# Seven block products for eight pairs of gated units in the second layer of a two-layer decoder step

## The chip, the cores and the metric

The kernel runs on one core of a Trainium2 chip. The metric is the device time of one execution in microseconds (us); lower is better. In the profile PE is TensorE's matmul side and PEld its weight loads, DVE is VectorE, ACT is ScalarE, POOL is GpSimd, and SP is the engine that issues most DMAs.

## The reference, cut to what matters

Two layers run over 520 positions (512 of a prompt, 8 single-position samples) with 1024 channels. The first layer is a convolution mixer; the change leaves its arithmetic alone. The second is a gated MLP with a spatial mix:

```python
def c_mixer(x, w_in, w_s, b_s, norm_v_g, norm_v_b, w_out):
    z = jnp.einsum('bld,de->ble', x, w_in)          # D_MODEL 1024 -> 3 x 2048
    u, v, g = jnp.split(z, (D_C, 2 * D_C), axis=-1)
    u = jax.nn.gelu(u)
    v = layer_norm(jax.nn.gelu(v), norm_v_g, norm_v_b)
    ...
    w_causal = w_s * jnp.tril(jnp.ones((CHUNK, CHUNK), w_s.dtype))
    mix = jnp.einsum('hts,bnshd->bnthd', w_causal, vc) + jnp.transpose(b_s)[None, None, :, :, None]
    ...
    y = u * mix * jax.nn.silu(g)
    return jnp.einsum('ble,ed->bld', y, w_out), v

# every layer: x <- LayerNorm(alpha * x + sublayer(x))
```

All data are fp32.

## The kernel before, in words

**Layout.** Channels lie on the 128 partitions and positions on the free axis, so an activation of 1024 channels is eight tiles of 128 x 520. The weights come as *units*: 1024 input channels by 128 output channels, a tile of 128 x 1024 in SBUF, one DMA of 512 KB each. There are 136 units, in the order in which they are used: first layer 0 to 71 (the last eight, 64 to 71, are its second output projection), then v 72 to 87, then for each half of the 2048 gated channels four u, four g, four u, four g (88 to 103 and 112 to 127), and eight units of the output projection (104 to 111, 128 to 135).

**Exact products.** Each fp32 operand is split into two fp32r parts, a rounded one (`whi`, `x1h`) and the rest (`wlo`, `x1l`). `whi` is a cast on ACT (L121), `wlo` a subtraction on DVE (L128); for units 10 to 49 it is an accumulating DMA instead. A product of a unit takes three matmuls (hi by hi, lo by hi, hi by lo) for each of 8 blocks of input channels and each half of 260 positions: 48 matmuls of 128x128 by 128x260, in `mm2` (L157). `mm` (L142) does one half of the positions, 24 matmuls.

**Order.** `unit(n)` (L137) sees to it that the weights of the next `LEAD` = 5 units have been asked for. The parts live in 12 slots of the tag W; the raw weights in 3 of the tag `raw`. The instruction order of every engine is laid down by the framework when the kernel is built, by priorities (program order, raised by `soon()`, lowered by `background()`) and by its own estimate of times. On the chip each engine runs its list in order and waits on semaphores; a slot is taken again when its last reader is done. SP's queue, which issues all raw loads, is such a list too.

**PSUM.** `zps` holds two tiles of two banks (`zt`), `cps` two of one bank, `mps` two for small things such as transposes and mixes.

**Second layer.** Sixteen v units: product, GELU, then `v_tok` (L616): four transposes on TensorE, an ACT copy to an SBUF tile (L622), statistics on DVE. All 16 transposed tiles stay in SBUF (in slots that the first layer used for `cA` and `sB`). `v_finish` (L655), called after the first u unit, makes mean and scale and normalizes the 64 blocks of v in place on DVE (L663). `c_group` (L733) does four u units (GELU on ACT, L741, into `gu`) and then four g units (SiLU on ACT, L756). `mix_unit` (L710) is eight small matmuls on v and a DVE pass (L722); `split_y` makes the product with `mix` (L405) and its two fp32r parts (ACT cast L406, DVE L407), `yh` and `yl`. After eight channel blocks, `z_q` multiplies them by the output projection and the partial sums stay in SBUF as `r1` (L773, L776). After the other eight, `out_part` (L478 on) does the second projection (`z_p`) in two halves of the positions, adds it to the kept sum on DVE (L492), and normalizes.

The temporaries have tags of their own: T (`tmp`, 7 slots), B (`btmp`, 4 slots, which hold `gu`), Y (17 slots), M (4 slots).

Of the kernel before, what the change touches and what calls it, by code (L numbers as in the profile page):

```python
# [9 lines left out]
F32 = mybir.dt.float32  # L10
# [31 lines left out]

LEAD = 5
CUT = 260
# [6 lines left out]
def decoder_kernel(  # L51
# [27 lines left out]
    zps = ctx.enter_context(tc.tile_pool(name="zps", bufs=2, space=bass.MemoryType.PSUM))  # L79
    mps = ctx.enter_context(tc.tile_pool(name="mps", bufs=2, space=bass.MemoryType.PSUM))  # L80

    def xs_slot(dt, name):
# [4 lines left out]

    def ab_slot(name):
        return slots.tile([P, T], F32, tag="AB", name=name, bufs=8)

# [21 lines left out]

    n_units = 2 + wu.shape[0]
    units = [None, None]

    def load_unit(wtag=("W", 12)):
        n = len(units)
        raw = wpool.tile([P, KT, P], F32, tag="raw", name=f"raw_{n}", bufs=3)
        nc.sync.dma_start(raw, wu[n - 2])
        hi = wpool.tile([P, KT, P], F32R, tag=wtag[0], name=f"whi_{n}", bufs=wtag[1])  # L120
        nc.scalar.copy(hi, raw)  # L121
        lo = wpool.tile([P, KT, P], F32R, tag=wtag[0], name=f"wlo_{n}", bufs=wtag[1])
        if n in BY_DMA:

            nc.scalar.mul(lo, raw, -1.0)  # L125
            nc.gpsimd.dma_start(lo, wu[n - 2], accum_op=ALU.add)  # L126
        else:
            nc.vector.tensor_tensor(lo, raw, hi.bitcast(F32), op=ALU.subtract)  # L128
        units.append((hi, lo))


    BY_DMA = set(range(10, 50))
    EXTRA = set()
    for base in (64, 128):
        EXTRA.update((base + 6, base + 7))

    def unit(n):  # L137
        while len(units) < min(n + 1 + LEAD, n_units):
            load_unit(("M", 4) if len(units) in EXTRA else ("W", 12))
        return units[n]  # L140

# [14 lines left out]

    def mm2(z, w, ah, al):  # L157
        hi, lo = w
        for k in range(KT):
            for h in range(2):  # L160
                for j, (a, b) in enumerate(((hi, ah), (lo, ah), (hi, al))):
                    nc.tensor.matmul(  # L162
                        z[h][:, :TH],
                        a[:, k, :],
                        b[k][:, hs(h)],
                        start=(k == 0 and j == 0),
                        stop=(k == KT - 1 and j == 2),
                    )
# [15 lines left out]
    for k in range(KT):  # L184
        x = tmp(f"x_{k}")
        if k % 4 == 0:
            raw = wpool.tile([P, 4, 2, P], F32, tag="raw", name=f"raw_s{k}", bufs=3)
            w0h.append(wpool.tile([P, 4, 2, P], F32R, tag="W", name=f"whi_s{k}", bufs=12))
            w0l.append(wpool.tile([P, 4, 2, P], F32R, tag="W", name=f"wlo_s{k}", bufs=12))
        q, j = k // 4, k % 4  # L190
# [28 lines left out]

    load_unit()  # L220
    pa = const.tile([P, KT, NPA], F32, name="pa")
# [13 lines left out]


    unit(1)
    xs = []
    for j in range(2):
        t = wpool.tile([P, 4, NS, WA], F32, tag="M", name=f"xs_{j}", bufs=4)  # L240
        nc.sync.dma_start(t, cache_a[:, 4 * j : 4 * j + 4])
        xs.append(t)
# [45 lines left out]
    for i in range(KT):  # L288
# [24 lines left out]
        nc.gpsimd.dma_start(cap_out[:, i, :], ap[:, SEQ : SEQ + PADA])  # L313
        cA.append(ab_slot(f"cA_{i}"))
        if i % 2 == 1:
# [16 lines left out]
        nc.gpsimd.dma_start(cbp_out[:, i, :], ch[:, SEQ : SEQ + PADB])  # L332
        s = slots.tile([P, T], F32, tag="SB", name=f"sB_{i}", bufs=8)
        sB.append(s)
# [24 lines left out]
    with background():  # L359
        for j in range(2):  # L360
            nc.gpsimd.dma_start(cas_out[:, 4 * j : 4 * j + 4], xs[j])
            proda = wpool.tile([P, 4, NS, WA], F32, tag="M", name=f"proda_{j}", bufs=4)
# [95 lines left out]
    for d in range(KT):  # L458
        xr = tmp(f"xr_{d}")
        nc.sync.dma_start(xr, xT[:, d, :])  # L460
        r = slots.tile([P, T], F32, tag="SB", name=f"r_{d}", bufs=8)
        if d == 2:
# [15 lines left out]
    def out_part(base, c0, c1, yh, yl, res, lnc, done, last=False, pool_sub=()):  # L478
# [39 lines left out]
        def norm():  # L518
# [26 lines left out]
            for d in range(KT):  # L545
# [3 lines left out]
                if last:  # L549
                    if d % 4 == 0:  # L550
                        out = wpool.tile([P, 4, nn], F32, tag="raw", name=f"out_{d}", bufs=3)
                    o = out[:, d % 4, :]
# [38 lines left out]

    wt = wpool.tile([P, NH, P], F32, tag="M", name="wt", bufs=4)
    nc.gpsimd.dma_start(wt, wsT_in)
    bs = wpool.tile([P, NH, P], F32, tag="M", name="bs", bufs=4)
    nc.gpsimd.dma_start(bs, bs_in)
# [17 lines left out]
    vs = tiny.tile([P, NV, NS], F32, name="vs")  # L613
    stats = wpool.tile([P, NC, NV, 6], F32, tag="M", name="stats", bufs=4)

    def v_tok(i):  # L616
        nc.gpsimd.tensor_copy(vs[:, i, :], vt[i][:, SEQ:])
        m = mt(f"vt_{i}")
        for c in range(NC):
            nc.tensor.transpose(m[:, c * P : (c + 1) * P], vt[i][:, c * P : (c + 1) * P], ident)  # L620
        t = ab_slot(f"vtok_{i}") if i < 8 else slots.tile([P, T], F32, tag="SB", name=f"vtok_{i}", bufs=8)
        nc.scalar.copy(t[:, :SEQ], m)  # L622
# [19 lines left out]
    for i in range(NVF, NV):  # L642
        z = zt(f"z_v{i}")
        mm2(halves(z), unit(n + i), x1h, x1l)
        vt[i] = y_slot(F32, f"v_{i}")
        nc.scalar.activation(two(vt[i]), zh(z), AF.Gelu_apprx_tanh)
        v_tok(i - 1)
    n += NV

    mv = tiny.tile([P, NC, 2], F32, name="mv")  # L650
    rs = tiny.tile([P, NC], F32, name="rs")
    mixs = tiny.tile([P, NV, NS], F32, name="mixs")
    rowsum = wpool.tile([P, NH, P], F32, tag="M", name="rowsum", bufs=4)

    def v_finish():  # L655
# [4 lines left out]
        nc.gpsimd.tensor_tensor(rs, rs, neg_half[:, :NC], op=ALU.pow)  # L660
        for i in range(NV):
            for c in range(NC):
                nc.vector.tensor_scalar(  # L663
                    vtok[i][:, c * P : (c + 1) * P],
                    vtok[i][:, c * P : (c + 1) * P],
                    mv[:, c, 0:1],
                    rs[:, c : c + 1],
                    op0=ALU.subtract,
                    op1=ALU.mult,
                )  # L670

# [37 lines left out]

    def mix_unit(i):  # L710
        h = i // 2
# [5 lines left out]
        for c in range(NC):  # L717
            nc.tensor.matmul(  # L718
                m[:, c * P : (c + 1) * P], vtok[i][:, c * P : (c + 1) * P], wt[:, h, :], start=True, stop=True
            )  # L720
# [10 lines left out]
        return t  # L731

    def c_group(g0):  # L733
        nonlocal n
        gu = []
        for i in range(g0, g0 + 4):
            z = zt(f"z_u{i}")
            mm2(halves(z), unit(n), x1h, x1l)
            n += 1
            t = btmp(f"gu_{i}")  # L740
            nc.scalar.activation(two(t), zh(z), AF.Gelu_apprx_tanh)  # L741
            gu.append(t)
            if i == 0:
                v_finish()

        def finish(i):
            t = gu[i - g0]
            split_y(i, t, mix_unit(i), "c", 1)

        for i in range(g0, g0 + 4):  # L750
            z = zt(f"z_gc{i}")
            mm2(halves(z), unit(n), x1h, x1l)
            n += 1
            g = tmp(f"silu_c{i}")
            t = gu[i - g0]
            nc.scalar.activation(two(g), zh(z), AF.Silu)  # L756
            nc.vector.tensor_tensor(t, g, t, op=ALU.mult)
            if g0 > 0:
                finish(i)
        if g0 == 0:  # L760
            for i in range(4):
                finish(i)

    yh, yl = [], []
    c_group(0)
    c_group(4)
    res = []
    for d in range(KT):
        z = zt(f"z_q{d}")
        mm2(halves(z), unit(n), yh, yl)  # L770
        n += 1
        r = ab_slot(f"r1_{d}")
        nc.vector.scalar_tensor_tensor(  # L773
# [3 lines left out]
            r, x1l[d].bitcast(F32), ALPHA, r, op0=ALU.mult, op1=ALU.add  # L777
        )
        res.append(r)
    yh, yl = [], []  # L780
    c_group(8)
    c_group(12)

# [108 lines left out]
```

## Time and profile before

| what | us |
|---|---|
| time, median of 3 runs (lowest, highest) | 834.26 (833.76, 834.76) |
| the profiled execution, its own time | 834.73 |
| its span, first to last instruction | 833.0 |
| v units, the stretch from 424.8 to 526.8 | 102.0 |
| first half of u and g units, 526.8 to 627.3 | 100.5 |
| `z_q`, 627.3 to 673.3 | 46.0 |
| second half of u and g units, 673.3 to 771.9 | 98.7 |
| `z_p`, then the last LayerNorm, 771.9 to 833.0 | 61.1 |

The page gives each engine's busy time over the span; the chain that ended last lists, in order of time, what the end of the kernel hung on. A matmul's duration in a group of instructions is its latency: consecutive matmuls overlap, so a rate has to be read from the start and the length of a piece of the chain, divided by its count.

### The profile page before, as it was taken

To read this page: it belongs to the slowest core of one execution; us is meant where nothing else is said; L and a number is where in the kernel's file an instruction comes from. 1 tells how busy PE (TensorE), PEld (TensorE's weight loads), DVE (VectorE), ACT (ScalarE), POOL (GpSimd) and SP (SyncE) were. 2 spreads that over 40 slices of the span, in tenths; PEclk is the share of its full clock that TensorE was granted. 3 is DMA by queue.
4 is the path that set the end of the run, shared out by engine and by line. 5 is a ranking of instruction groups with operands and counts; after the bars stand their busy time and mean duration, and the time that the engine had idled before them with its cause. 6 is when DMAs were issued, how large, how long until landed. Compare 5 with 4: busy or idle time off the path is not lost.

```text
span 833.0 us, 16028 instructions
## 1 busy us (share of the span) xinstructions
PE 814.2 (98%) x6792; PEld 812.2 (98%) x6792; DVE 536.6 (64%) x914; ACT 347.2 (42%) x510; POOL 88.0 (11%) x158
## 2 busy tenths in 40 slices
PE   8999999999999999999989999999999999999994
PEld 8999999999999999999979999999999999999993
DVE  5899998999962576446885432596355433526566
ACT  5545454455354444442647423323432133334243
POOL 0121221221110000000021111100000000000032
PEclk9999999999999999999989999999999999999997
DMA  8798988889888543231331432214233223222011
GB/s 290 208 206 191 209 185 185 184 191 216 182 173 189 167 115 102 79 124 52 84 119 51 128 85 93 77 56 126 78 87 92 84 94 102 77 87 92 1 53 52
DMA packets 32873, 103.37 MB, mean 124 GB/s; under 512 B 4209, under 2 KB 7937, under 8 KB 32801
## 3 DMA queue, kind: packets, MB, share of 16 engines
q1 hardware_dynamic: 26000, 79.01, 32.2%
q0 software_dynamic: 6800, 23.33, 15.0%
q8 instruction: 53, 0.87, 0.4%
q14 instruction: 20, 0.16, 0.1%
HBM read 98.89 MB, written 3.44 MB: 123 GB/s over the span
## 4 chain that ended last, share of the span: by engine, by line
PE 96%; DMA 1%; DVE 1%; ACT 0%; SPq 0%; issue 0%; ACTq 0%; DVEq 0%
PE z_p L146 11%; PE z_gc L162 11%; PE z_u L162 11%; PE z_v L162 7%; PE z_q L162 6%; PE z_o L162 6%; PE z_c L162 5%; PE z_ga L162 5%; PE z_post L162 5%; PE z_h L162 5%; PE z_gb L162 5%; PE z_val L162 5%; PE z_gate L162 5%; PE z_v L146 5%; PE mix L718 2%; PE vt L620 1%
## 5 line engine op out<-in xcount | busy, mean ns | idle before, releaser
L121 ACT CAST whi<-raw 128x1024 fp32r<-128x1024 f32 x134 | 139.9, 1048 | 324.9 <-PE z_u L162 44.9
L128 DVE TENSOR_TENSOR wlo<-raw,whi 128x1024 fp32r<-128x1024 f32 x94 | 114.4, 1224 | 142.5 <-ACT whi L121 141.9
L274 DVE SCALAR_TENSOR_TENSOR acc<-apad,pa,acc 128x512 f32<-128x512 f32 x240 | 165.7, 751 | 3.6 <-ACT acc L271 2.7
L162 PE MATMUL z_gc<-x1h,whi 128*128 128x260 f32 x256 | 72.9, 285 | 0.0
L162 PE MATMUL z_u<-x1h,whi 128*128 128x260 f32 x256 | 72.4, 283 | 0.0
L162 PE MATMUL z_gc<-x1h,wlo 128*128 128x260 f32 x256 | 72.0, 281 | 0.0
L162 PE MATMUL z_u<-x1l,whi 128*128 128x260 f32 x256 | 72.0, 281 | 0.0
L162 PE MATMUL z_gc<-x1l,whi 128*128 128x260 f32 x256 | 72.0, 281 | 0.0
L162 PE MATMUL z_u<-x1h,wlo 128*128 128x260 f32 x256 | 72.0, 281 | 0.0
L126 POOL DMA_DIRECT2D wlo<-in_wu x40 | 34.7, 869 | 139.2 <-ACT wlo L125 132.2
L162 PEld LDWEIGHTS z_u<-x1h,wlo 128*128 128x128 f32 x256 | 48.1, 188 | 0.1
L162 PEld LDWEIGHTS z_gc<-x1h,wlo 128*128 128x128 f32 x256 | 48.2, 188 | 0.0
L162 PEld LDWEIGHTS z_gc<-x1l,whi 128*128 128x128 f32 x256 | 48.1, 188 | 0.0
L162 PEld LDWEIGHTS z_u<-x1h,whi 128*128 128x128 f32 x256 | 48.0, 188 | 0.1
L162 PEld LDWEIGHTS z_u<-x1l,whi 128*128 128x128 f32 x256 | 48.1, 188 | 0.0
L162 PEld LDWEIGHTS z_gc<-x1h,whi 128*128 128x128 f32 x256 | 48.1, 188 | 0.0
L162 PE MATMUL z_v<-x1h,whi 128*128 128x260 f32 x160 | 46.0, 287 | 0.0
L162 PE MATMUL z_v<-x1h,wlo 128*128 128x260 f32 x160 | 45.0, 281 | 0.0
L162 PE MATMUL z_v<-x1l,whi 128*128 128x260 f32 x160 | 45.0, 281 | 0.0
L125 ACT ACTIVATE wlo<-raw 128x1024 fp32r<-128x1024 f32 x40 | 42.2, 1055 | 0.0
L162 PE MATMUL z_c<-xh,wlo 128*128 128x260 f32 x128 | 36.1, 282 | 0.3 <-DVE wlo L128 0.3
L146 PE MATMUL z_p<-yh_c,whi 128*128 128x260 f32 x128 | 36.3, 284 | 0.0
(260 smaller groups left out, 2723.4 us busy)
## 6 DMA issues: line engine op xcount, KB each, us to landing
raw<-in_wu SPq DMA_DIRECT2D x134, 512.0 KB, 3.9
wlo<-in_wu POOLq DMA_DIRECT2D x40, 512.0 KB, 7.7
xr<-in_xT SPq DMA_DIRECT2D x8, 260.0 KB, 4.2
x<-in_xT SPq DMA_DIRECT2D x7, 260.0 KB, 5.1
out_y<-r SPq DMA_DIRECT2D x8, 130.0 KB, 1.7
out_y<-out SPq DMA_DIRECT2D x4, 260.0 KB, 2.2
raw_s<-in_w SPq DMA_DIRECT2D x8, 128.0 KB, 4.5
xs<-in_cache_a SPq DMA_DIRECT2D x2, 496.0 KB, 8.2
```

The source lines that it names most:

```text
L121: nc.scalar.copy(hi, raw)
L125: nc.scalar.mul(lo, raw, -1.0)
L126: nc.gpsimd.dma_start(lo, wu[n - 2], accum_op=ALU.add)
L128: nc.vector.tensor_tensor(lo, raw, hi.bitcast(F32), op=ALU.subtract)
L146: nc.tensor.matmul(ps, a[:, k, :], b[k][:, c], start=(k == 0 and j == 0), stop=(k == KT - 1 and j == 2),)
L162: nc.tensor.matmul(z[h][:, :TH], a[:, k, :], b[k][:, hs(h)], start=(k == 0 and j == 0), stop=(k == KT - 1 and j == 2),)
L274: nc.vector.scalar_tensor_tensor(acc[i], apads[i][:, j : j + SEQ], pa[:, i, PA_W + j : PA_W + j + 1], acc[i], op0=ALU.mult, op1=ALU.add,)
L620: nc.tensor.transpose(m[:, c * P : (c + 1) * P], vt[i][:, c * P : (c + 1) * P], ident)
L718: nc.tensor.matmul(m[:, c * P : (c + 1) * P], vtok[i][:, c * P : (c + 1) * P], wt[:, h, :], start=True, stop=True)
```

## The change

Two units that lie next to each other in u or in g, and the x they multiply, are seen as 2x2 blocks: two blocks of output channels, two of 512 input channels (a11, a12 for the first unit, a21, a22 for the second), two of 260 positions (b). Instead of eight block products of 12 matmuls each, seven are made, after Strassen, in Winograd's form. This is done for the second pair of each four units, so 8 of 16 pairs; each lies between two plain units. The four sums of weights for such a pair, S1 to S4, are made on DVE from the raw weights, and each is split into hi and lo like a plain unit; the four sums of x (`x_forms`) are made once, during the v units, and kept in 16 slots. The seven products run p1, p5, p6, p2, p7; then half of the next plain unit; then p4 and p3 (`land`); then the rest of that plain unit. They accumulate in two PSUM banks, out of which partial sums are copied by ACT and added by DVE in between. To make room, the transposed v goes to DRAM (a DMA on POOL's queue for each of 16) and comes back on SP's queue by `fetch` when its g pair begins; its normalization happens then, half on DVE and half on ACT. `r1` goes to DRAM and back as well. Slots are cut anew: `cA`, `sB`, `r` and the x sums share a tag R of 16, `raw` has 4, M has 3, the statistics lie in Y; the weights ahead are counted in slots (`AHEAD` = 10; a plain unit counts 2, a pair 7).

The core of the diff:

```diff
+    def load_pair(n1, n2):
+        r1, r2 = load_raw(n1), load_raw(n2)
+        a1 = parts(n1, r1)
+        a22 = w_slot(f"wa22_{n1}", (P, 2, 4, P))
+        nc.scalar.copy(a22[:, 0], r2[:, 4:])
+        nc.vector.tensor_tensor(a22[:, 1], r2[:, 4:], a22[:, 0].bitcast(F32), op=ALU.subtract)
+        nc.vector.tensor_tensor(r2[:, :4], r2[:, :4], r2[:, 4:], op=ALU.add)
+        nc.vector.tensor_tensor(r1[:, :4], r1[:, :4], r2[:, :4], op=ALU.add)
+        nc.vector.tensor_tensor(r2[:, 4:], r1[:, :4], r2[:, 4:], op=ALU.subtract)
+        s13 = parts(n2, r2, kind="s")
+        nc.vector.tensor_tensor(r1[:, 4:], r1[:, 4:], r1[:, :4], op=ALU.add)
+        s24 = parts(n1, r1, kind="s")
...
     def v_tok(i):
...
-        t = ab_slot(f"vtok_{i}") if i < 8 else slots.tile([P, T], F32, tag="SB", name=f"vtok_{i}", bufs=8)
-        nc.scalar.copy(t[:, :SEQ], m)
+        t = tmp(f"vtok_{i}")[:, :SEQ]
+        nc.scalar.copy(t, m)
...
-        vtok[i] = t
+        vtok[i] = spill.tile([P, SEQ], F32, name=f"vd_{i}")
+        nc.gpsimd.dma_start(vtok[i], t)
...
+    def x_forms(k):
...
+        nc.vector.tensor_tensor(f[0], b11, b12, op=ALU.subtract)
+        nc.vector.scalar_tensor_tensor(f[1], f[0], -1.0, b22, op0=ALU.mult, op1=ALU.subtract)
+        nc.vector.tensor_tensor(f[2], b22, b12, op=ALU.subtract)
+        nc.vector.scalar_tensor_tensor(f[3], f[1], -1.0, b21, op0=ALU.mult, op1=ALU.subtract)
+        for j in range(4):
+            t = r_slot(f"xf{j}_{k}", F32R, (P, 2, TH))
+            nc.scalar.copy(t[:, 0], f[j])
+            nc.vector.tensor_tensor(t[:, 1], f[j], t[:, 0].bitcast(F32), op=ALU.subtract)
...
+    def product(ps, a, b, first=False):
+        for k in range(4):
+            (ah, al), (bh, bl) = a(k), b(k)
+            for j, (p, q) in enumerate(((ah, bh), (al, bh), (ah, bl))):
+                nc.tensor.matmul(ps, p, q, start=(first and k == 0 and j == 0), ...)
...
+    class Seven:
...
+        def copy(self, out, src):
+            with soon():
+                nc.scalar.copy(out, src)
+        def add(self, out, src):
+            with soon():
+                nc.vector.tensor_tensor(out, out, src, op=ALU.add)
+        def p1(self):
+            self.w = need(*self.job)
+            z = zt(f"z_{self.key}")
+            self.b1, self.b2 = z[:, 0, :TH], z[:, 1, :TH]
+            product(self.b1, self.w["a11"], self.x(0, 0), True)
+            self.copy(self.c1[:, hs(0)], self.b1)
+        def p5(self):
+            product(self.b2, self.w["s1"], self.f(1), True)
+        def p6(self):
+            product(self.b1, self.w["s2"], self.f(2))
+            self.copy(self.c1[:, hs(1)], self.b1)
+        def p2(self):
+            b3 = cps.tile([P, SEQ], F32, tag="cv", name=f"z_{self.key}_2")[:, :TH]
+            product(b3, self.w["a12"], self.x(1, 0), True)
+            self.add(self.c1[:, hs(0)], b3)
+        def p7(self):
+            product(self.b1, self.w["s3"], self.f(3))
+            self.copy(self.c22, self.b1)
+            self.add(self.c22, self.b2)
+        def p4(self):
+            product(self.b1, self.w["a22"], self.f(4))
+        def p3(self):
+            product(self.b2, self.w["s4"], self.x(1, 1))
+            self.add(self.c1[:, hs(1)], self.b2)
...
     def v_finish():
...
-        for i in range(NV):
-            for c in range(NC):
-                nc.vector.tensor_scalar(vtok[i][...], ..., mv[:, c, 0:1], rs[:, c : c + 1], ...)
...
+    def fetch(i):
+        t = tmp(f"vback_{i}")[:, :SEQ]
+        nc.sync.dma_start(t, vtok[i])
+        for c in range(NC):      # c < 2: tensor_scalar on DVE; else Identity with scale and bias on ACT
...
+    def c_pair(m, tag, out, func, last):
+        u, w = (out(f"{tag}_{m + j}") for j in range(2))
+        if (m, m + 1) in place:
+            def mid(z):
+                with soon():
+                    nc.scalar.activation(w[:, hs(0)], z, func, scale=-1.0)
+            def end():
+                nc.scalar.activation(u, u, func)
+                nc.scalar.activation(w[:, hs(1)], w[:, hs(1)], func, scale=-1.0)
+                last(u, w)
+            step(Seven(f"{tag}{m}", (m, m + 1), u, w[:, hs(1)]), mid, end)
+            return
+        for j, t in enumerate((u, w)):
+            z = zt(f"z_{tag}{m + j}")
+            mm2(halves(z), unit(m + j), x1h, x1l, range(KT // 2))
+            if j == 0:
+                for _ in land():       # p4, mid, p3, end of the pair before
+                    pass
+            mm2(halves(z), unit(m + j), x1h, x1l, range(KT // 2, KT))
+            with soon():
+                nc.scalar.activation(two(t), zh(z), func)
+        last(u, w)
...
     for d in range(KT):
         z = zt(f"z_q{d}")
...
-        r = ab_slot(f"r1_{d}")
+        r = tmp(f"r1_{d}")
...
+        t = spill.tile([P, T], F32, name=f"rd_{d}")
+        nc.gpsimd.dma_start(t, r)
...
+    for d in range(KT):
+        r = r_slot(f"r2_{d}")
+        nc.sync.dma_start(r, r1[d])
+        res.append(r)
```

More of the change, by code (lines that the diff above doesn't have):

```diff
@@ L132, in decoder_kernel @@
     BY_DMA = set(range(10, 50))
-    EXTRA = set()
+    EXTRA = {}
     for base in (64, 128):
-        EXTRA.update((base + 6, base + 7))
+        EXTRA[base + 6] = ("M", "M")
+        EXTRA[base + 7] = ("M", "raw")
+    JOBS = [(n,) for n in range(2, 88)]
+    for half in range(2):
+        base = 88 + 24 * half
+        for m in range(base, base + 16, 4):
+            JOBS += [(m,), (m + 1,), (m + 2, m + 3)]
+        JOBS += [(n,) for n in range(base + 16, base + 24)]
+    place = {job: j for j, job in enumerate(JOBS)}
@@ L137, in unit, with need @@
+    loaded = []
+    def need(*job):
+        j = place[job]
+        ahead = lambda: sum(2 if len(q) == 1 else 7 for q in JOBS[j + 1 : len(loaded)])
+        while len(loaded) < len(JOBS) and (len(loaded) <= j or ahead() < AHEAD):
+            q = JOBS[len(loaded)]
+            loaded.append(load_unit(*q) if len(q) == 1 else load_pair(*q))
+        return loaded[j]
     def unit(n):
-        while len(units) < min(n + 1 + LEAD, n_units):
-            load_unit(("M", 4) if len(units) in EXTRA else ("W", 12))
@@ L140, in unit @@
-        return units[n]
+        return need(n)
     def mm(ps, w, ah, al, c):
@@ L234, in decoder_kernel @@
     nc.gpsimd.memset(neg_half, -0.5)
-    unit(1)
+    loaded.extend(load_unit(m) for m in range(3, 7))
     xs = []
     for j in range(2):
-        t = wpool.tile([P, 4, NS, WA], F32, tag="M", name=f"xs_{j}", bufs=4)
+        t = wpool.tile([P, 4, NS, WA], F32, tag="M", name=f"xs_{j}", bufs=3)
         nc.sync.dma_start(t, cache_a[:, 4 * j : 4 * j + 4])
@@ L550, in norm @@
                     if d % 4 == 0:
[L551 removed]
+                        out = wpool.tile([P, 4, nn], F32, tag="raw", name=f"out_{d}", bufs=NRAW)
                     o = out[:, d % 4, :]
@@ new lines, in product, with __init__, x, f @@
+    def product(ps, a, b, first=False):
+        for k in range(4):
+            (ah, al), (bh, bl) = a(k), b(k)
+            for j, (p, q) in enumerate(((ah, bh), (al, bh), (ah, bl))):
+                nc.tensor.matmul(
+                    ps, p, q, start=(first and k == 0 and j == 0), stop=(k == 3 and j == 2),
+                    skip_group_check=True,
+                )
+    class Seven:
+        def __init__(self, key, job, c1, c22):
+            self.key, self.job, self.c1, self.c22 = key, job, c1, c22
+        def x(self, half, h):
+            return lambda k: (x1h[4 * half + k][:, hs(h)], x1l[4 * half + k][:, hs(h)])
+        def f(self, j):
+            return lambda k: (xf[j - 1][k][:, 0], xf[j - 1][k][:, 1])
+        def copy(self, out, src):
[28 more added lines that the diff above has]
+            self.add(self.c1[:, hs(1)], self.b2)
@@ L627, in decoder_kernel, with land, step @@
+    flight = [None]
+    def land():
+        if flight[0] is not None:
+            p, mid, end = flight[0]
+            p.p4()
+            mid(p.b1)
+            yield
+            p.p3()
+            end()
+            flight[0] = None
+        yield
+    def step(p, mid, end):
+        p.p1()
+        p.p5()
+        prev = land()
+        next(prev)
+        p.p6()
+        next(prev, None)
+        p.p2()
+        p.p7()
+        flight[0] = p, mid, end
     for i in range(NVF):
@@ L731, in mix_unit @@
         return t
-    def c_group(g0):
[L734 to L743, printed above, removed]
-                v_finish()
[L746 to L762, printed above, removed]
+    back = {}
@@ new lines, in c_group, with gated_pair, last @@
+    def c_group(g0):
+        m = 88 + g0 // 8 * 24 + g0 % 8 // 4 * 8
+        us = []
+        for j in (0, 2):
+            c_pair(m + j, "u", btmp, AF.Gelu_apprx_tanh, lambda *t: us.extend(t))
+            if g0 + j == 0:
+                v_finish()
+        def gated_pair(e):
+            def last(*gs):
+                for j, g in enumerate(gs):
+                    finish(e + j, us[e + j - g0], g)
+            return last
+        for j in (0, 2):
+            back.update((g0 + j + o, fetch(g0 + j + o)) for o in range(2))
+            c_pair(m + 4 + j, "g", tmp, AF.Silu, gated_pair(g0 + j))
@@ L764, in decoder_kernel, with c_half @@
+    def c_half(half):
+        c_group(8 * half)
+        c_group(8 * half + 4)
+        for _ in land():
+            pass
     yh, yl = [], []
-    c_group(0)
-    c_group(4)
-    res = []
+    c_half(0)
+    r1 = []
     for d in range(KT):
         z = zt(f"z_q{d}")
-        mm2(halves(z), unit(n), yh, yl)
-        n += 1
-        r = ab_slot(f"r1_{d}")
+        mm2(halves(z), unit(104 + d), yh, yl)
+        r = tmp(f"r1_{d}")
         nc.vector.scalar_tensor_tensor(
```

111 lines of the change are left out of this document (72 added, 39 removed).

## The prediction

> **What bounds the kernel now.** I read first the busy shares and the chain that ended last, on the page: which engine sets the end.
>
> ```profile
> PE 814.2 (98%) x6792; PEld 812.2 (98%) x6792; DVE 536.6 (64%) x914; ACT 347.2 (42%) x510; POOL 88.0 (11%) x158
> PE 96%; DMA 1%; DVE 1%; ACT 0%; SPq 0%; issue 0%; ACTq 0%; DVEq 0%
> ```
>
> TensorE is busy for 98% and makes 96% of the chain. So I next read what PE ever waited for; the view has four rows, all of them in other places than the u and g units:
>
> ```profile
> PE z_v L146 <- DVE r L492: 4.1, 1, 4.1
> PE z_first L212 <- ACT xh L205: 1.2, 2, 1.0
> PE warm L175 <- DVE warm L172: 1.1, 1, 1.1
> PE z_c L162 <- DVE wlo L128: 0.3, 1, 0.3
> ```
>
> Then the chain in order of time, for the rate (start, length, piece):
>
> ```profile
> 673.25 22.85 PE z_u L162 x192
> 696.10 5.70 PE z_gc L162 x48
> 701.80 0.89 PE mix L718 x8
> 771.93 15.04 PE z_p L146 x125
> ```
>
> Four u units take 22.85 us for 192 matmuls: 0.119 us each, 5.71 us a unit. `z_p`, whose matmuls go one after another into one bank as those of a block product do, has 15.04 / 125 = 0.120, so the new form has no price of its own. Last, the stages by windows (length, then busy us and instructions of PE, PEld, DVE, ACT, POOL, granted clock, DMA share, GB/s):
>
> ```profile
> 18.20:189.60 171.40, 171.38 (x1441) 171.38 (x1442) 158.97 (x231) 84.01 (x104) 36.03 (x59) 1.00 0.88 199
> 465.00:526.50 61.50, 61.50 (x521) 61.50 (x520) 20.10 (x50) 19.87 (x31) 7.64 (x10) 1.00 0.31 94
> 526.50:575.00 48.50, 48.50 (x407) 48.33 (x406) 34.51 (x101) 16.36 (x22) 4.81 (x9) 1.00 0.29 89
> 575.00:627.20 52.20, 52.20 (x444) 52.20 (x443) 27.60 (x40) 19.62 (x26) 1.19 (x5) 1.00 0.28 81
> 673.20:771.90 98.70, 98.70 (x835) 98.70 (x834) 41.43 (x53) 36.32 (x45) 1.25 (x5) 1.00 0.28 86
> ```
>
> In the u and g stages (the last three rows) PE has no gap while DVE is busy for about half the time, ACT for a third. Matmuls taken away there shorten the span one for one, as long as what feeds TensorE keeps up.
>
> **The change part by part.** The durations come from these groups (minimum, median, maximum in ns, or on the page busy us and mean ns):
>
> ```profile
> L121 ACT CAST whi<-raw 128x1024 fp32r<-128x1024 f32 x134 | 139.9, 1048 | 324.9 <-PE z_u L162 44.9
> L128 DVE TENSOR_TENSOR wlo<-raw,whi 128x1024 fp32r<-128x1024 f32 x94 | 114.4, 1224 | 142.5 <-ACT whi L121 141.9
> L405 DVE TENSOR_TENSOR gu<-gu,mix x16: 691/696/702, 577.7 to 776.1; 128x520 f32<-128x520 f32 x16
> L492 DVE TENSOR_TENSOR r<-z_p,r x32: 412/428/434, 380.2 to 819.4; 128x260 f32<-128x260 f32 x32
> L663 DVE TENSOR_SCALAR vtok<-vtok,mv,rs 128x128 f32<-128x128 f32 x64 | 16.5, 363 | 0.4 <-POOL rs L660 0.4
> L622 ACT COPY vtok<-vt x16: 577/579/591, 454.4 to 533.9; 128x512 f32<-128x512 f32 x16
> L632 ACT COPY v<-z_v x6: 354/373/378, 431.6 to 449.1; 128x260 f32<-128x260 f32 x6
> L741 ACT ACTIVATE gu<-z_u x16: 599/601/607, 533.4 to 746.3; 128x520 f32<-128x520 f32 x16
> ```
>
> *Matmuls removed, on the path.* One block product of eight per pair, 12 matmuls, in 8 pairs: 96 x 0.119 = **-11.4 us**. Weight loads fall by the same 96 and lie beside the matmuls, as now.
>
> *Weight sums, beside.* A pair cost DVE 2 x 1.22 = 2.4 us; now three splits of 1.22, one of half the width and four sums of 128x512, each near 0.69 (the 128x520 row): 3.7 + 0.7 + 2.8 = 7.1, so +4.7. ACT goes from 2.1 to 3 x 1.05 + 0.58 = 3.7, +1.6. The cover is the time between two pairs. Slots: the pair running holds 7 of 12, the next two plain units 4, one is free. The next pair gets a1 and the S1/S3 parts by the end of p7 and the rest by the end of p4 and p3, which is half a unit plus a unit (2.85 + 5.71) before its own p1 and 2.85 more before p6. What cannot begin before p3 is two casts and two splits, 1.05 + 0.58 + 1.22 + 0.69 = 3.5 us, so cost 0; without that cover see the second rival.
>
> *Sums of x, beside.* 16 sums and 16 differences of 0.43 on DVE (13.8 us), 16 ACT casts near the copy's 0.37, in the v stage whose row shows DVE at 20.1 of 61.5. First needed two units after that stage: 0.
>
> *Hand-overs inside a pair, partly on the path.* p6 goes into the bank that ACT must first copy after p1, and p7 after p6; p5 and p2 stand between. The trace of before has no such turn; the nearest is the last projection, matmul to DVE and back to a weight load:
>
> ```profile
> 819.04 0.28 PE L146 MATMUL z_p<-yl_c,whi 128*128 128x260 f32 x1
> 819.37 0.43 DVE L492 TENSOR_TENSOR r<-z_p,r 128x260 f32<-128x260 f32 x1 [0.36 <-PE z_p L146]
> 819.85 0.39 PEld L523 LDWEIGHTS mean<-r,ones_r 128*128 128x128 f32 x2
> ```
>
> Each hand-over there takes 0.05. From the start of p1's last matmul: 0.28 + 0.05 + copy 0.37 + 0.05 = 0.75; the first matmul of p6 is due 13 x 0.119 = 1.55 after it. Slack 0.80, with ACT free. Behind a weight cast that has just begun (1.05) the copy would be 0.25 late, in 16 places 4.0 us at most; the lower end is 0, since ACT's idle share of the stage is now 63%, will still be some 40% (below), and the copies have priority. I take 0.05 each: **+0.8 us**, near the lower end because PE never once waited for ACT or DVE in this stage. p4 and p3 have half a unit as cover, which a copy and an add (0.37 + 0.43) fit in.
>
> *At the end of each half* that half unit is missing: p4 follows p7 and waits for the copy, p3 for the add behind it. Bounds 0 (PE has the first matmuls of the next projection to put there, as far as the built order does so) to 0.75 + 0.48 each; I take 0.3, twice: **+0.6**.
>
> *The second projection's start.* Now units 14 and 15 of `yh` are late together, not 15 alone. Before, TensorE ran on over that:
>
> ```profile
> 770.76 0.28 PE L162 MATMUL z_gc<-x1l,whi 128*128 128x260 f32 x1
> 772.55 0.59 ACT L756 ACTIVATE silu_c<-z_gc 128x520 f32<-128x520 f32 x1
> 777.52 0.70 DVE L407 TENSOR_TENSOR yl_c<-gu,yh_c 128x520 fp32r<-128x520 f32 x1 [0.75 <-ACT yh_c L406]
> ```
>
> The last part was ready at 778.2, 7.2 us after the last g matmul, at no PE wait: four of eight output tiles have a PSUM bank each, and their first seven blocks (4 x 21 matmuls, 10.1 us) need no unit 15. Now six blocks, 4 x 18 x 0.12 = 8.6, and two mixes (0.89 each) stand against about 8 (7.2 plus another 0.7 pass). Bounds 0 to 2; I take **+0.2**. The reloads of `r1` share SP's queue with the weights, and are due only when the first tile is done.
>
> *Moved, at no cost.* v's normalization leaves DVE's solid 16.5 us behind the first u unit (L663) and comes in 8 blocks a pair, half on ACT. The transfers of v and `r1`, two ways, are 12.6 MB; these rows are the nearest:
>
> ```profile
> raw<-in_wu SPq DMA_DIRECT2D x134, 512.0 KB, 3.9
> wlo<-in_wu POOLq DMA_DIRECT2D x40, 512.0 KB, 7.7
> xr<-in_xT SPq DMA_DIRECT2D x8, 260.0 KB, 4.2
> ```
>
> A fetched v is back in about 5 us and is needed 10 us or later, at the end of its pair (7 x 1.43 at the least), so it hides. On SP it waits for a T slot, and raw loads stand behind it; those run two units or more ahead. On POOL 24 issues stand behind the small copies `vs`; who waits is the T slot of a transposed v: by the 7.7 of the second row it is held some 9 us and one comes every 6.2 (below), so two of seven slots. DVE in the second half becomes 41.4 + 4 x 4.7 + 12 adds x 0.43 + 16 x 0.36 = 71 of 93 us (76%); in the first half 62.1 - 16.5 + 29.7 = 75 of 95. The convolution stage in the first window row runs DVE at 159.0 of 171.4 with no gap on PE, so 79% alone is no bound. The v cadence, from the chain:
>
> ```profile
> 477.46 5.73 PE z_v L162 x48
> 483.63 5.73 PE z_v L162 x48
> ```
>
> **Sum.** On the profiled execution, 834.73: -11.4 + 0.8 + 0.6 + 0.2 = -9.8, so 824.9; that execution is 0.47 above the median of 834.26, so **824.5** for the median.
>
> **The rivals.**
>
> *Hand-overs cost a cast each.* If the order built in advance puts a cast in front of most copies, or ACT runs late, 16 x 0.25 = 4.0, ends 2 x 1.23 = 2.5, projection 2.0: -11.4 + 8.5, 831.4. For it: ACT goes to about 60% (36.3 + 4 x 1.6 + 12 x 0.37 + 16 blocks of v near 0.5, over 93) and runs in order. Against: the empty list of waits. At 0.70 a hand-over the gain is gone and there is no change, about 834.
>
> *The pairs' weights come late: slower.* Place: p5 and p6 of a pair that follows a g pair, where DVE also has `split_y` and the mix passes of two units. If all seven slots' work began only after p3 of the pair before (DVE blocked at its head on a slot or a raw tile), 7.1 us of sums and splits plus 8.4 of finishing (8 passes of 0.7 for two units, 3 adds of 0.43, 4 blocks of v at 0.36) stand against 2.85 + 5.71 + 2.85 = 11.4: 4.1 late. In four such places 16.4: 834.3 - 11.4 + 16.4 = 839.3. It decides from 11.4 / 4 = 2.85 us per place. For it: two raw tiles of four are held until the last split, and DVE's sums overwrite `raw` in place, a chain in order. Against: a1 and S1/S3 have their slots 5.7 us earlier.
>
> A wait that long has a second price, seen between the layers:
>
> ```profile
> 424.83 0.56 PE L146 MATMUL z_v<-x1h,whi 128*128 128x260 f32 x1 [4.15 <-DVE r L492]
> 424.80:430.80 6.00, 5.97 (x27) 0.50 0.00 0
> ```
>
> After 4.15 us idle, TensorE ran for 6.0 us at a granted clock of 0.50: 27 matmuls where 50 would fit, 3 us lost. The Trainium skill ("TensorE: Matmul & The Clock Gate", section on the clock gate) states that an idle window of about 3.4 us halves the clock, and about as much activity restores it; the trace agrees in kind. By that rule the forecast's waits, all under 1 us, cost nothing further, while four waits of 4.1 would add some 12 us, to 851. The same page says that only weight loads are pulled ahead and matmuls stay in program order; by that rule a late p6 is paid in full, though work is ready behind it.
>
> *More than forecast.* If DVE's relief behind the first u unit or the new slots also remove waits, below 822.8; nothing in the view of PE's waits gives more than the 4.1 between the layers, which the change does not touch.
>
> **How the numbers follow.** Forecast (822.5 to 827.5): 0.60, for the stage without PE waits. Hand-overs (827.5 to 832.6): 0.18. No change, within 0.2% (1.7 us, about what a measurement of this kernel can tell): 0.07. Late weights, slower: 0.12. Below 822.5: 0.03. Faster: 0.60 + 0.18 + 0.03 = 0.81. The range runs from 822.0, the full 11.4 and a little, to 833.5, where the hand-over case ends in no change; it leaves out the late weights and part of no change.
>
> **What would show it.** PE's matmuls fall by about 96; four u or g units with a pair take 21.4 us on the chain, not 22.85. PE's waits on ACT's copies inside pairs stay under 1 us in all, and no wait on a weight split appears. The clock stays at 1.00 from 466 to the last projection. Wrong if the chain shows DVE's sums or ACT's copies in the u and g stages, or `z_p` waiting for `yl` of unit 15 or for a reloaded `r1`.

## The result and the profile after

The changed kernel took 845.99 us in the median of 4 runs (844.84 to 846.0) beside 834.01 (833.36 to 834.76) for the kernel before: a ratio of 1.014, 95% interval 1.0122 to 1.0157. It is slower by 12 us, where 9.8 us less had been forecast. The profiled execution took 844.84 with a span of 843.1.

In the line numbers of the changed kernel, `product` is L707, a plain unit's matmul L215, the copies and adds of a pair L728 and L732, its activations on landing L921 (`mid`), L924 and L925 (`end`), a plain unit's activation, which empties its z tile, L938; weight casts are L126, their differences L133.

The busy line and the chain of the page:

```profile
PE 810.1 (96%) x6696; PEld 804.9 (95%) x6696; DVE 579.8 (69%) x987; ACT 406.1 (48%) x622; POOL 105.1 (12%) x182
PE 90%; DVE 3%; ACT 3%; DMA 2%; issue 1%; SPq 1%; ACTq 0%; DVEq 0%
```

The 96 matmuls are gone (6792 to 6696), yet PE is 96% busy, and 10% of the chain lies on other engines, where it was 4%. What PE waited for, the view that had four rows:

```profile
PE z_g L707 <- ACT g L938: 5.8, 2, 3.0
PE z_v L199 <- DVE r L545: 4.0, 1, 4.0
PE z_u L215 <- ACT u L938: 3.0, 2, 1.5
PE z_g L707 <- ACT g L921: 2.4, 2, 1.9
PE z_p L199 <- ACT yh_c L459: 1.3, 1, 1.3
PE warm L228 <- DVE warm L225: 1.1, 1, 1.1
PE z_q L215 <- DVE g L732: 0.9, 1, 0.9
...
PE z_u L215 <- ACT g L938: 0.6, 1, 0.6
PE z_p L199 <- DVE g L732: 0.5, 1, 0.5
...
```

The rows with L938 are new in kind: a product, a pair's or a plain unit's, waits for ACT to empty *another* unit's z tile. The windows (length, then busy us and count of PE, PEld, DVE, ACT, POOL, granted clock, DMA share, GB/s): the v units from 465, then from each half the stretch with these waits, five microseconds of the first, and the two projections:

```profile
465.00:525.70 60.70, 60.70 (x515) 60.70 (x514) 33.08 (x87) 24.63 (x46) 11.36 (x20) 1.00 0.39 125
577.00:625.90 48.90, 44.44 (x348) 43.89 (x347) 28.82 (x48) 31.50 (x45) 2.92 (x4) 0.93 0.34 108
615.00:620.00 5.00, 5.00 (x25) 5.00 (x25) 3.35 (x7) 4.99 (x11) 0.00 (x0) 0.51 0.21 74
728.00:772.50 44.50, 40.16 (x331) 39.42 (x330) 28.19 (x46) 30.82 (x44) 1.78 (x4) 1.00 0.34 112
625.90:677.50 51.60, 49.87 (x410) 49.25 (x410) 29.55 (x41) 14.08 (x17) 3.78 (x7) 1.00 0.39 124
772.50:843.10 70.60, 54.62 (x439) 53.01 (x437) 46.86 (x96) 26.59 (x53) 11.47 (x15) 0.94 0.21 73
```

The v units carry the x sums and the spill with no gap. In the u and g stretches PE idles for 4.5 and 4.3 us. `z_q` takes 51.6 us where it took 46.0 (2.9 of that is p4 and p3 of the last pair, which land there), the second projection with its LayerNorm 70.6 where it took 61.1.

What stands in ACT's list at the longest wait (timeline of ACT: start, us, instruction):

```profile
609.23 1.05 ACT L126 CAST whi<-raw 128x1024 fp32r<-128x1024 f32 x1 [1.53 <-PE z_g L215]
610.30 1.28 ACT L925 ACT_TABLE_LOAD   x1
611.59 0.42 ACT L925 ACTIVATE u<-u 128x260 f32<-128x260 f32 x1
612.03 1.28 ACT L938 ACT_TABLE_LOAD   x1
613.32 0.60 ACT L938 ACTIVATE g<-z_g 128x520 f32<-128x520 f32 x1
613.94 1.28 ACT L921 ACT_TABLE_LOAD   x1
615.24 0.39 ACT L921 ACTIVATE u<-z_u 128x260 f32<-128x260 f32 x1
```

and PE's at the same time:

```profile
609.03 0.28 PE L215 MATMUL z_g<-x1l,whi 128*128 128x260 f32 x1
...
609.39 1.61 PE L707 MATMUL z_u<-xf,wa 128*128 128x260 f32 x12
613.98 0.58 PE L707 MATMUL z_g<-x1h,whi 128*128 128x260 f32 x1 [2.98 <-ACT g L938]
```

The plain g unit is complete at 609.3. ACT gets to its tile at 613.32: ahead stand a weight cast and the GELU of the u pair that is landing, and since GELU and SiLU lie in different tables, that one activation costs two loads of 1.28. The u pair holds the other z tile until it has landed, so p1 of the g pair has no tile to go to before 613.9. The clock of 0.51 in the third window belongs to this wait: half clock ran from 613.11 to 619.93.

The groups of table loads in the u and g stages, in the kernel before:

```profile
L756 ACT ACT_TABLE_LOAD x4 | 5.1, 1283 | 0.1
L741 ACT ACT_TABLE_LOAD x3 | 3.8, 1283 | 0.1
```

and in the changed kernel:

```profile
L938 ACT ACT_TABLE_LOAD x11 | 14.1, 1283 | 0.9 <-PE z_g L215 0.7
L925 ACT ACT_TABLE_LOAD x8 | 10.3, 1283 | 0.1
L924 ACT ACT_TABLE_LOAD x2 | 2.6, 1283 | 0.0
L921 ACT ACT_TABLE_LOAD x2 | 2.6, 1283 | 0.0
```

7 loads became 23: the activations of a landing u pair fall among g units and the other way round. The Trainium skill ("ScalarE: Activation LUTs", What ACT_TABLE_LOAD costs) gives 1283 ns for the load, as here, and about 1380 ns of drain on top; no drain shows in the timeline above, where one instruction starts within 0.02 us of the end of the one before.

**Where 21.5 us lie** (843.1 against 833.0 - 11.4), by the gaps of over 0.3 us between the starts of successive matmuls, less 0.12 each: in the u and g stages five waits, with one slow matmul behind the longest, 10.5; the first end 2.2 (0.76, 1.22, 0.59); the second 4.8 (2.20, 0.80, 1.62, 0.45, 0.32); 26 matmuls at half clock at 0.22 for 0.12, 2.6. Together 20.1; the rest is in smaller gaps.

### The profile page after: what moved, and what is told of

It reads as the page before. It is cut to its first block, busy times and chain, and to the rows that moved or that the text cites. A ratio compares the mean times of both kernels' runs of the same rounds, so it can differ in the third digit from the quotient of the medians.

```text
span 843.1 us, 16157 instructions
## 1 busy us (share of the span) xinstructions
PE 810.1 (96%) x6696; PEld 804.9 (95%) x6696; DVE 579.8 (69%) x987; ACT 406.1 (48%) x622; POOL 105.1 (12%) x182
## 4 chain that ended last, share of the span: by engine, by line
PE 90%; DVE 3%; ACT 3%; DMA 2%; issue 1%; SPq 1%; ACTq 0%; DVEq 0%
PE z_p L199 8%; PE z_v L215 7%; PE z_u L215 6%; PE z_o L215 5%; PE z_c L215 5%; PE z_g L215 5%; PE z_gb L215 5%; PE z_ga L215 5%; PE z_post L215 5%; PE z_h L215 5%; PE z_q L215 5%; PE z_val L215 5%; PE z_gate L215 5%; PE z_v L199 4%; PE z_u L707 4%; PE z_g L707 4%
## 5 line engine op out<-in xcount | busy, mean ns | idle before, releaser
L126 ACT CAST whi<-raw 128x1024 fp32r<-128x1024 f32 x126 | 131.5, 1047 | 233.5 <-PE z_post L215 25.0
L133 DVE TENSOR_TENSOR wlo<-raw,whi 128x1024 fp32r<-128x1024 f32 x86 | 104.7, 1222 | 92.9 <-ACT whi L126 63.8
L215 PE MATMUL z_v<-x1h,whi 128*128 128x260 f32 x160 | 45.9, 287 | 0.0
L215 PE MATMUL z_v<-x1l,whi 128*128 128x260 f32 x160 | 45.1, 282 | 0.0
L215 PE MATMUL z_v<-x1h,wlo 128*128 128x260 f32 x160 | 45.0, 281 | 0.0
L215 PE MATMUL z_u<-x1h,whi 128*128 128x260 f32 x128 | 36.8, 287 | 3.6 <-ACT u L938 3.0
L133 DVE TENSOR_TENSOR slo<-raw,shi 128x1024 fp32r<-128x1024 f32 x16 | 19.6, 1224 | 29.2 <-ACT shi L126 16.2
L215 PE MATMUL z_q<-yh_c,whi 128*128 128x260 f32 x128 | 36.4, 285 | 1.3 <-DVE g L732 0.9
L215 PE MATMUL z_g<-x1h,whi 128*128 128x260 f32 x128 | 36.3, 284 | 0.0
L199 PE MATMUL z_p<-yh_a,wlo 128*128 128x260 f32 x128 | 36.3, 284 | 0.0
L215 PE MATMUL z_u<-x1h,wlo 128*128 128x260 f32 x128 | 36.2, 283 | 0.0
L199 PE MATMUL z_p<-yl_a,whi 128*128 128x260 f32 x128 | 36.2, 284 | 0.0
L215 PE MATMUL z_q<-yh_c,wlo 128*128 128x260 f32 x128 | 36.1, 283 | 0.0
L215 PE MATMUL z_gb<-xh,whi 128*128 128x260 f32 x128 | 36.1, 282 | 0.0
L215 PE MATMUL z_c<-xh,wlo 128*128 128x260 f32 x128 | 36.1, 282 | 0.0
L215 PE MATMUL z_g<-x1h,wlo 128*128 128x260 f32 x128 | 36.1, 282 | 0.0
L199 PE MATMUL z_p<-yh_a,whi 128*128 128x260 f32 x128 | 36.1, 282 | 0.0
L215 PE MATMUL z_q<-yl_c,whi 128*128 128x260 f32 x128 | 36.0, 283 | 0.0
```

Of the source, the lines that this page charges most:

```text
L199: nc.tensor.matmul(ps, a[:, k, :], b[k][:, c], start=(k == 0 and j == 0), stop=(k == KT - 1 and j == 2),)
L215: nc.tensor.matmul(z[h][:, :TH], a[:, k, :], b[k][:, hs(h)], start=(k == 0 and j == 0), stop=(k == KT - 1 and j == 2),)
```

## The experiments

My theory had two causes: (a) ACT empties the one free z tile late, (b) the last pair of each half lands without cover. Rivals: the moved parts cost something, or DVE's and ACT's extra work eats the gain as such.

**No pairs at all, everything else kept** (the same spill and reloads, slots, x sums and queues).

```diff
-            JOBS += [(m,), (m + 1,), (m + 2, m + 3)]
+            JOBS += [(m,), (m + 1,), (m + 2,), (m + 3,)]
```

> No pair at all: 16 plain pairs, with everything else of the change kept (sums of x made and not used, v and r1 through DRAM, the new slots, later normalization). Theory: the moved parts cost nothing by themselves: 833 to 836. Rival 'the moves cost': the transfers, the blocked SP queue or the fewer temporaries stall TensorE: 838 to 846.

833.94 (833.08 to 834.77), ratio to before 1.0001 (0.9991 to 1.001). What was moved costs nothing; all of the loss belongs to the pairs.

**One function for u and g.** ACT loses 22 loads, and the u units hold another function's values; the order of PE, ACT and DVE is that of the changed kernel.

```diff
-            c_pair(m + j, "u", btmp, AF.Gelu_apprx_tanh, ...)
+            c_pair(m + j, "u", btmp, AF.Silu, ...)
```

> SiLU stands in for GELU in the u units (that part of the result is left out); the order of all engines is that of the changed kernel except that the 22 function-table loads of the u and g stages are gone. Theory 'tables': while a pair is in flight only one of the two z tiles is left for plain units, so TensorE waits for evictions on ACT, and those stand behind table loads of 1.28 us; the waits of PE on ACT (11.8 us) and the stretch at half clock (2.5 us lost) mostly go: 846 - 8 to 12, so 834 to 838. Rival 'late weights' (sums and splits of the pairs and the projections' units come late, loads only fill idle time of ACT): 845 to 846.

832.84 (832.13 to 834.36), ratio 0.9989 (0.998 to 0.9998): about 13 us less than the changed kernel, a little more than expected. What PE waited for, without two rows that every version has and two of 0.3 and 0.2:

```profile
PE z_g L707 <- ACT g L921: 2.3, 2, 1.8
PE z_p L199 <- ACT yh_c L459: 1.3, 1, 1.3
PE z_q L215 <- DVE g L732: 0.9, 1, 0.9
PE z_p L199 <- DVE g L732: 0.8, 1, 0.8
```

All rows with L938 are gone (four gaps of 0.3 to 0.4 are left there), those of the ends remain. The loads make the waits of the u and g stages here, 10.5 + 2.6 by the gaps above, by themselves or together with the single tile; later runs take these apart.

**Fewer loads by order.** The landing's activations are tied together and the plain unit's behind them; 7 loads are left.

```diff
+                with tc.issue_after(mid_act[0]):
+                    first = nc.scalar.activation(u, u, func).ins
...
-            with soon():
+            with soon(), (tc.issue_after(landed[0]) if landed[0] is not None else nullcontext()):
                 nc.scalar.activation(two(t), zh(z), func)
```

> Nothing left out: a landing pair's three activations are issued one behind the other, and the next plain unit's activation behind them, so that 8 table loads are left in the u and g stages instead of 24 (7 before the change). 'Tables': most of what the run with one function gains, but evictions now also wait for the landing: 834 to 840. 'Late weights': 845 to 847.

852.32 (850.14 to 853.29), ratio 1.0217 (1.0199 to 1.0235): a miss, slower still. The longest of its new waits:

```profile
PE z_g L215 <- DVE u L732: 6.0, 3, 2.4
```

A plain unit's tile is now emptied only after the landing, so the next unit waits for the pair's own tile, which the landing's last add on DVE frees. The number of loads is not the measure; what counts is how long a tile is held, whatever its emptying waits behind.

**The last g pair of each half as two plain units** (six pairs, functions as they are).

```diff
+            last_pair = m == base + 12
-            JOBS += [(m,), (m + 1,), (m + 2, m + 3)]
+            JOBS += [(m,), (m + 1,)] + ([(m + 2,), (m + 3,)] if last_pair else [(m + 2, m + 3)])
```

> The last g pair of each half is two plain units (6 pairs of seven products instead of 8; 24 matmuls or 2.9 us more). Theory 'ends': what TensorE loses at the starts of z_q (2.2 us of gaps) and z_p (4.8 us) comes from a pair that ends a half, which holds 7 of 12 weight slots and lands uncovered while the projection's units are to be loaded: those gaps go, so 846 + 2.9 - 7.0 = 842, less if the 3.1 us waits just ahead of these two pairs go as well (then about 834). Rival: the ends are late because DVE and ACT are behind from the whole stage; then the gaps stay and it is 847 to 849.

833.37 (832.85 to 834.72), ratio 0.9997 (0.9987 to 1.0006). At the starts of `z_q` and `z_p` one gap of 0.44 is left, and the two waits of about 3 us ahead of the last g pairs are gone, with the half clock at one of them; gaps of 0.4 to 1.8 remain in the u and g stages. Two of these are of a kind that the changed kernel does not show there: a product of a pair waits for ACT's copy out of its own bank (`PE z_u L708 <- ACT u L729: 1.4, 2, 0.7`).

**Both: one function and six pairs.**

> The last g pair of each half is two plain units (six pairs), and the u units take SiLU instead of GELU (their values are therefore another function's), so that ACT loads no table in the u and g stages. Theory (the table loads and the uncovered ends are the two causes, and the seven products themselves pay as counted): the kernel with no pairs had 833.9; 72 matmuls fewer x 0.119 = -8.6 gives 825.3, and the small gaps left in the u and g units when only the table loads were gone, about 2.4 us for 8 pairs, add 1.8: 827 (825 to 829). Rival (the sums and splits load DVE and ACT so much that the products gain little): 831 or more.

827.72 (826.57 to 827.85), ratio 0.9929 (0.9914 to 0.9944) to the 833.53 of this group: as expected. The largest gap in the u and g stages is 0.36.

**The single tile, with all loads kept.** The second plain unit sums in the two single banks of `cps`.

```diff
-            z = zt(f"z_{tag}{m + j}")
+            if j == 0:
+                z = zt(f"z_{tag}{m + j}")
+                zz = halves(z)
+            else:
+                zz = [cps.tile([P, SEQ], F32, tag="cv", name=f"z_{tag}{m + j}_{h}") for h in range(2)]
...
+                    for h in range(2):
+                        nc.scalar.activation(t[:, hs(h)], zz[h][:, :TH], func)
```

> Eight pairs and all table loads as in the changed kernel, but the second plain unit of each couple takes the two single banks of the other pool for its sums instead of a z tile, so that the z tile which a pair in flight leaves free is not asked for twice in a row. Theory (a table load costs only because the next product waits for the one free z tile to be emptied by ACT): the gaps ahead of z_u and z_g at L707/L215 in the u and g stages, 10.8 us with the 2.5 us at half clock behind one of them, go to about 2; the ends stay: 834 to 837. Rival (the landing's own activations, or ACT's queue as such, hold PE): 843 to 846.

831.48 (830.64 to 832.66), ratio 0.9976 (0.9966 to 0.9985): some 14 us less than the changed kernel, more than expected, with 23 loads still in the u and g stages. The built order shifts with the second tile, unlike in the run with one function, so this is the worth of the tile together with the order that it allows. The stretch of the first half that had the waits, then some three microseconds at the second end:

```profile
577.00:618.00 41.00, 41.00 (x348) 41.00 (x347) 28.09 (x46) 29.11 (x44) 2.21 (x4) 1.00 0.38 117
774.40:777.70 3.30, 3.30 (x17) 3.24 (x16) 2.54 (x4) 1.15 (x2) 0.00 (x0) 0.50 0.00 0
```

As many matmuls, 348, take 41.0 us with no idle time, where they took 48.9. What it still loses lies at the ends: gaps of 0.75, 1.22 and 0.59, and of 1.16, 2.43, 0.34 and 0.44, with the half clock of the second row behind them.

**The control: the kernel before with its functions mixed.**

```diff
-            nc.scalar.activation(two(t), zh(z), AF.Gelu_apprx_tanh)
+            nc.scalar.activation(two(t), zh(z), (AF.Gelu_apprx_tanh, AF.Silu)[i % 2])
...
-            nc.scalar.activation(two(g), zh(z), AF.Silu)
+            nc.scalar.activation(two(g), zh(z), (AF.Gelu_apprx_tanh, AF.Silu)[i % 2])
```

> The kernel before, with GELU and SiLU taken in turn by unit in both the u and the g units (half of them are therefore another function's), so that ACT loads tables 29 times where it loaded 7; the order on PE is that of before. Theory (a table load of 1.28 us costs nothing while a second z tile is free): 834 (833.3 to 836). Rival (a table load delays PE wherever it stands): 22 x about 0.6 us, 13 us as in the changed kernel: 845 or more.

834.0, ratio 1.0003 (0.9993 to 1.0013). Its loads in the u and g stages:

```profile
L756 ACT ACT_TABLE_LOAD x16 | 20.5, 1283 | 0.3
L741 ACT ACT_TABLE_LOAD x15 | 19.2, 1283 | 0.3
```

31 loads, 40 us of ACT, cost nothing while two tiles take turns.

**Six pairs, SiLU from Tanh.** Tanh shares GELU's table, so no load stands in the stage and the functions are the reference's; DVE reads z as well, one more pass a unit (`cut(ue(j))` is the unit's u).

```diff
+            nc.vector.scalar_tensor_tensor(
+                cut(ue(j)), cut(ue(j)), 0.5 * s, z, op0=ALU.mult, op1=ALU.mult
+            )
+            nc.scalar.activation(o, z, AF.Tanh, scale=0.5 * s)
...
-        nc.vector.tensor_tensor(u, u, g, op=ALU.mult)
+        nc.vector.scalar_tensor_tensor(u, g, 1.0, u, op0=ALU.add, op1=ALU.mult)
```

> Six pairs as in the run without the last pairs, and g's SiLU made as 0.5 x (1 + tanh(x/2)): Tanh shares GELU's table, so no load stands in the u and g stages, and the result is the reference's. DVE reads z as well (u x z, 16 more passes of 0.7 us). Theory: as the run with one function and six pairs, 825 to 829; DVE's extra 11 us over 195 us lie beside PE. Rival (emptying a g tile now hangs on DVE's queue, behind splits of 1.22 and sums, and PE waits there instead): 831 to 838.

830.12 (829.16 to 831.26), ratio 0.9962 (0.9949 to 0.9975): between the theory's 829 and the rival's 831. Two gaps of 1.42 ahead of a plain u unit behind a landing and one of 0.75 remain. Emptying a tile hangs on two engines here: ahead of the first of these gaps DVE's reading stands behind a weight split of 1.23, and Tanh then behind a cast of 0.62 on ACT.

**The remedies together: six pairs and the single banks**, functions and loads as they are.

> Both remedies together, with the reference's functions and all their table loads: the second plain unit sums in the two single banks, and the last g pair of each half is two plain units (six pairs). Theory (one free z tile, and landings without cover, are the whole loss): 833.5 of the kernel before - 72 x 0.119 = 824.9, plus 1 for small gaps: 826 (825 to 828). Rival (something else of the pairs' work costs as well): 829 or more.

826.45 (825.83 to 827.68), ratio 0.9912 (0.9898 to 0.9927) to 833.8. The busy line and all that PE waited for:

```profile
PE 806.7 (98%) x6720; PEld 804.9 (98%) x6720; DVE 571.6 (69%) x969; ACT 406.9 (49%) x624; POOL 104.1 (13%) x182
```

```profile
PE z_v L200 <- DVE r L546: 3.9, 1, 3.9
PE warm L229 <- DVE warm L226: 1.1, 1, 1.1
PE z_c L216 <- DVE wlo L133: 0.3, 1, 0.3
```

The view is as empty as before the change, with 27 loads in the stage and DVE and ACT as busy as in the changed kernel. The span fell by 8.9 (833.0 to 824.1), the median by 7.4, for 72 x 0.119 = 8.6; 825 to 828 had been expected. This version beats both kernels, and the rival that the extra work eats the gain falls.

**Eight pairs, each in the middle of its four** (plain, pair, plain), so that a pair lands inside a unit of its own kind: with single banks, with Tanh on two z tiles, and with neither.

```diff
-            JOBS += [(m,), (m + 1,), (m + 2, m + 3)]
+            JOBS += [(m,), (m + 1, m + 2), (m + 3,)]
```

> Eight pairs, each in the middle of its four units (plain, pair, plain), so that every pair lands inside a plain unit of the same kind, and that plain unit sums in the single banks. Theory (as above; half a plain unit of 2.85 us and five eighths of the first unit of the projection, 3.6, now stand behind the last landing of a half, against about 10 us of DVE passes for three units): the gaps at the starts of z_q and z_p, 2.6 and 4.8 us in the changed kernel, fall to 1 or 2 each; 833.5 - 11.4 + 3 = 825 (823 to 828). Rival (the end of a half needs plain units for more than that): as with the gaps left, 829 or more.

> Eight pairs in the middle of their fours, on the two z tiles as in the changed kernel, and SiLU made from Tanh so that no table is loaded in the u and g stages. Theory (without loads the one free z tile costs 0.3 to 1.4 us a turn, as in the two runs without loads): 833.5 - 11.4 + 3 for the ends + 3 to 5: 829 (826 to 832). Rival (the turn of the tile is harmless without loads, and what was left in the run with Tanh were two accidents of order): 825.

> Only the place of the pairs changed: each in the middle of its four units, on the two z tiles, with GELU and SiLU as they are; in the built order the loads in the u and g stages fall from 24 to 16, since some landings still slip past the end of their plain unit. Theory (a load costs only where it stands between a product's end and the next one that wants the same tile): loads and ends both smaller but not gone: 834 (830 to 839). Rival (the place of the landing makes no difference while one tile has to serve): 843 or more.

With the banks 831.58 (ratio 0.9979, 0.9969 to 0.9988), with Tanh 849.55 (1.0184, 1.0167 to 1.0201), with neither 851.37 (1.0204, 1.0185 to 1.0223). All three missed. The banks are again worth 20 us; about 7 of these are the clock, since the version with neither runs 17 us at half clock between 600 and 800 (75 matmuls, each some 0.1 late) and the one with the banks none. Even so the ends keep gaps of 1.53, 0.41 and 0.59, and of 1.95, 1.36 and 0.45: p4 and p3 of the last pair came after the first matmuls of the projection in the built order, so the plain unit was no cover. In the version with neither, the largest waits are these:

```profile
PE z_g L215 <- ACT u L922: 6.4, 2, 3.2
PE z_p L199 <- DVE g L732: 3.2, 1, 3.2
PE z_q L215 <- ACT g L922: 2.6, 1, 2.6
```

There (L922 empties a plain unit's tile) a cast of 1.04, a copy of 0.37 and a load of 1.28 stand ahead. Without loads, in the version with Tanh, the same place still waits 1.8, behind cast and copy. So loads are the largest thing in that queue, not a condition of the wait. How much of the loss of the version with Tanh is DVE's second reading of z was not separated; some 3.6 us of it are half clock, which ran there for 10.2 us (36 matmuls).

## Why the prediction was wrong

**The step that failed is "Hand-overs inside a pair".** It was the sum's only price for a hand-over in the u and g stages. It priced the bank that passes from p1 to p6 to p7, and took 0.05 each "because PE never once waited for ACT or DVE in this stage". That emptiness was a property of two z tiles in turn: a finished tile had a whole unit, 5.7 us, to be emptied in. The change lends one of the two to a pair for as long as it is in flight, so every other product of that time hangs on the other tile. The sum had no term for it; it measured 10.5 us of gaps and 2.6 of half clock, and some 14 us came back when the second tile did. For the turn that it did price it held: a pair's bank makes no wait in the u and g stages of the changed kernel, nor in the six-pair version with the banks. Other orders did show such waits, 1.4 us in two with six pairs on two z tiles and 1.1 in three in the middle version with neither.

**The rival "Hand-overs cost a cast each" came nearest** (ACT in order, casts in front, 60% busy; it was 58%, 57.87 of 100.2 us, over the first half's u and g units and 64% in the window from 577), but at 831.4 it looked at the pair's own copies, and left out the loads. The 7 loads of 1283 ns were in the profile before, and nothing in the working counted them anew though two functions now land among each other's units.

**"At the end of each half" and "The second projection's start"** were right in place and mis-sized. For the two landings +0.6 stood against 4.5 (0.64 + 1.10 and 2.08 + 0.68), for the projection's start +0.2 against 2.0 (1.50 + 0.33 + 0.20); 0.47 in `z_q` had no term. The waits were not quite those named: p3 waited for ACT's activation of p4's bank (L921), not for the add, and the next projection tile for the last add (L732). At the second end the chain runs

```profile
774.07 6.38 DMA raw<-in_wu
780.44 0.02 issue
780.46 1.06 ACT whi L126
781.52 0.02 issue
781.55 1.24 DVE wlo L133
...
789.22 0.63 ACT yh_c L459
```

The raw weights of the projection are asked for late. On SP's queue the load of 774.07 stands behind the eight reloads of `r1`:

```profile
770.06 3.91 SPq L987 DMA_DIRECT2D r<-rd  x8
774.07 4.32 SPq L121 DMA_DIRECT2D raw<-in_wu  x2
```

The reloads go into slots of the x sums, which the last g pair still uses at that time (SP waits for PE's `z_g` four times, 2.4 us in all). The load of 778.05 then waits for a raw tile. The splits of these weights stand in DVE's list among the finishing passes of units 14 and 15, and the activation that p3 waits for stands on ACT behind a cast of weights that land at 782.5. The step counted the finishing and a PSUM bank for each of four tiles, but not the weights of those tiles, and it saw the reloads as due late, not as standing ahead of weights. How the 4.8 us divide between these was not separated. So the second rival's late weights did come, at a place that it did not name. Taking out the last pair of each half gave about 5 us (831.48 to 826.45 in the versions with the banks): the two cost some 8 us where their 24 matmuls save 2.9.

**"Weight sums, beside" and the second rival:** no PE wait on a weight split shows in the u and g stages; the cover was enough there. **"Moved, at no cost"** held without pairs, at 833.94; with them the reloads of `r1` are in the way at the second end, as above. **"Matmuls removed"** held: 96 fewer, and the rate of the gain is shown by the six-pair version. **The clock** did not stay at 1.00: 0.51 from 615 to 620, with the wait of 2.98.

## What to carry to other kernels

An empty list of waits says only that the slack before was enough. When a change holds an accumulator over other units' work, count the tiles left to those units, and price the emptying of each by all that can stand ahead of it on its engine, casts and table loads too, against the time until the next product wants that tile. Give a step that lands late a unit of other work behind it, and see in the built order that it stays there.

## What the runs showed of the hardware

Half clock came with shorter waits than I had assumed. In the changed kernel it set in during the wait of 2.98 us, but the like wait of 2.86 in the second half, the gap of 3.14 between starts, had none (the window from 728 has 1.00); in the version with the banks it followed gaps of 1.16 and 2.43 with twelve matmuls between them.

The length of the wait alone does not decide. In each trace all stretches of half clock start on one grid with steps of 3.41 us: in the middle version with neither at 601.32, 628.63, 754.92 and 789.05, which are 8, 37 and 10 steps apart. By these traces what decides is the idle time of PE within one step. The wait of 2.98 put 2.1 us of idle time into the step that ends at 613.11, and half clock begins there; the wait of 2.86 was cut by the edge of a step into 1.45 and 1.40. From 380 to 822 us of all 14 traces, every step with 2.04 us of idle time or more was followed by half clock and no step with 1.86 or less was; of two near 2.0 one was.

The Trainium skill ("TensorE: Matmul & The Clock Gate", section on the clock gate) puts it at an idle window of about 3.4 us that runs freely. The grid agrees with a window that runs freely, but in these runs some 2 us of idle time within it were enough. The wait of 2.1 us in the version with the banks cost some 1.3 us more in this way and that of 2.98 in the changed kernel 2.6, while that of 2.86 cost nothing more.
